# MLP down projection of a decoder layer: seven block products in place of eight

## The chip, the cores and the metric

The kernel runs on one core of a Trainium2 chip. The metric is the time of one execution in microseconds (us): the median of three runs of the kernel before is 2969.28 us (2967.07 to 2970.88).

The core has five engines with their own instruction queues: PE (TensorE, matrix products), DVE (VectorE), ACT (ScalarE), POOL (GpSimd) and SP (SyncE, which here only issues DMAs). Each queue is worked off in order; an instruction that has to wait holds up all that stand behind it on the same engine. Sixteen DMA engines move the data, whichever queue issued the transfer.

## The reference, cut to what matters

A decoder layer on 512 tokens with 2,048 features: three token mixers (a gated delta net, window attention, cross-attention to a memory), merged with gates and projected, then a squared-ReLU MLP with 8,192 hidden features. All in float32. The change is in the last line:

```python
h2 = rms_norm(x, mlp_norm_w[l])
x = x + jnp.square(jax.nn.relu(h2 @ w_mlp_up[l])) @ w_mlp_down[l]
```

`w_mlp_up` is 2048 x 8192 and `w_mlp_down` is 8192 x 2048. The output is `x`, 512 x 2048.

## The kernel before, in words

The kernel streams every weight matrix once from DRAM, in tiles of 256 rows by 512 columns (512 KB), laid out as 128 partitions x 2 x 512 in the tile `raw`. A float32 product is made of three products in a narrower form: each operand is split into a high part and a remainder, and `mm3` (L111 to L113) adds high x high, high x low and low x high into the same PSUM bank. One matmul has a 128 x 128 stationary operand and 512 moving columns.

So each weight tile goes through the same three steps before PE can use it: SP loads it (`wload`, L92; four `raw` buffers), ACT casts it into `whi` (L100; three buffers) and DVE forms the remainder `wlo` (L102; three buffers). A load waits until the buffer's last reader is done, the cast waits for a free `whi`.

The MLP runs in eight trips (`e_` from 0 to 7), each over 1,024 hidden features. In a trip, `feat_major` forms the hidden features in two halves of 512: eight weight tiles for each half, 24 matmuls for a tile, four PSUM accumulators `fa`. Each accumulator goes through ReLU on ACT (L929), a square on DVE (L930) and the split into `u_h` and `u_l` (L933, L934). Then `tok_major` runs the down projection: for each of four column groups of 512, four weight tiles of 24 matmuls each into four accumulators `ta`, one for each 128 tokens, and four DVE instructions (L939) that add the scaled accumulators to the residual `x1`. That makes 16 up tiles and 16 down tiles, 384 + 384 matmuls, in a trip. In the last trip the finished `x1` tiles are written out.

The order of instructions on each engine is set when the kernel is built, by a scheduler that puts ready instructions in the program's order as far as buffers allow. The hardware then follows that order.

Of the kernel before, what the change touches and what calls it, by code (L numbers as in the profile page):

```python
# [7 lines left out]
F32 = mybir.dt.float32  # L8
F32R = mybir.dt.float32r
BF16 = mybir.dt.bfloat16  # L10
AF = mybir.ActivationFunctionType
ALU = mybir.AluOpType
AX = mybir.AxisListType

P = 128
# [17 lines left out]
N_SLOTS = 75  # L33
YA, YB, YC, YX, YM = 10, 9, 5, 4, 14


@with_exitstack
def tile_layer(ctx: ExitStack, tc: tile.TileContext, a, out: bass.AP):
# [10 lines left out]
    def T(name, dt=F32, shape=(P, 512)):  # L49
        return big.tile(list(shape), dt, tag="T", bufs=N_SLOTS, name=name)  # L50
# [12 lines left out]

# [1 line left out]
    ident = const.tile([P, P], F32, name="ident")  # L65
# [19 lines left out]
    def rsqrt(out_ap, in_ap, n):  # L85
        nc.gpsimd.tensor_tensor(out=out_ap, in0=in_ap, in1=mhalf[:, :n], op=ALU.pow)

# [1 line left out]
    def wload(src, n):  # L89
        raw = wp.tile([P, 2, n], F32, tag="raw", bufs=4, padded_shape=[P, 2, 512], name="raw")  # L90
        if len(src.shape) == 3:
            nc.sync.dma_start(out=raw, in_=src)  # L92
        else:
            for k in range(2):
                nc.sync.dma_start(out=raw[:, k, :].rearrange("p (a b) -> p a b", b=src.shape[3]), in_=src[:, k])
        return wsplit(raw, n)
# [8 lines left out]
    def rows(w, k0, c0, n):  # L105
        return w[k0:k0 + 2 * P, c0:c0 + n].rearrange("(k p) c -> p k c", p=P)
# [8 lines left out]
    def feat_major(srcs, act, nacc):  # L115
        """out[a] = (W[:, a-th 128 columns])^T act; act[k] = (hi, lo) of [128 features, 512 tokens]."""
        accs = [acc_tile("fa") for _ in range(nacc)]
        ng_ = len(srcs)
        for g, s in enumerate(srcs):
            hi, lo = wload(s, nacc * P)  # L120
            for j in range(nacc):
                for k in range(2):
                    ah, al = act[2 * g + k]
                    c = slice(j * P, (j + 1) * P)
                    mm3(accs[j], hi[:, k, c], lo[:, k, c], ah, al, g == 0 and k == 0, g == ng_ - 1 and k == 1)
                pump()
# [21 lines left out]

# [1 line left out]
    bg = []  # L150
# [14 lines left out]

# [1 line left out]
    hm = []  # L167
# [60 lines left out]

    # remaining constants
    cm = const.tile([P, 5, P], F32, name="cm")  # L230
# [18 lines left out]

# [1 line left out]
    hT = []  # L251
# [85 lines left out]

# [1 line left out]
    toep = []  # L339
# [36 lines left out]
    for g in range(8):  # L376
        raw = wp.tile([P, 2, 268], F32, tag="raw", bufs=4, padded_shape=[P, 2, 512], name="raw")
        nc.sync.dma_start(out=raw[:, :, 0:12], in_=rows(w_in, 256 * g, COL_BA, 12))
        nc.sync.dma_start(out=raw[:, :, 12:268], in_=rows(w_in, 256 * g, COL_SK, 256))
        hi, lo = wsplit(raw, 268)  # L380
        for t in range(4):
            for k in range(2):
                ah, al = hT[2 * g + k]
                c = slice(t * P, (t + 1) * P)
                mm3(accs[t][:, :268], ah[:, c], al[:, c], hi[:, k, :], lo[:, k, :], g == 0 and k == 0, g == 7 and k == 1)
        pump()
# [17 lines left out]
    def decay():  # L404
        """beta = sigmoid(b); g = -exp(A_log) softplus(a + dt_bias); tokens on partitions."""
        bb, xa, na = th_("bb"), th_("xa"), th_("na")
# [78 lines left out]

# [1 line left out]
    def q_stats(qt):  # L487
        """rsqrt(mean(q^2) + eps) / sqrt(d) per token, [128, 4]."""
        sq = T("sq")
        nc.scalar.activation(out=sq, in_=qt, func=AF.Square)  # L490
        sp = sm("sp", (P, 4))
        for t in range(4):
            nc.tensor.matmul(sp[:, t:t + 1], lhsT=sq[:, t * P:(t + 1) * P], rhs=ones[:, 0:1], start=True, stop=True)  # L493
        ms = small("q_ms", 4, bufs=3)
        nc.vector.tensor_scalar(out=ms, in0=sp, scalar1=1.0 / HD, scalar2=EPS, op0=ALU.mult, op1=ALU.add)
        rq = small("q_r", 4, bufs=3)
        rsqrt(rq, ms, 4)
        nc.vector.tensor_scalar(out=rq, in0=rq, scalar1=SCALE, scalar2=None, op0=ALU.mult)
        return rq
# [100 lines left out]

# [1 line left out]
    def dn_head(h, raws, z, zg):  # L602
# [42 lines left out]

        # q statistics, token-major keys and values
        sq = raws[0]
# [128 lines left out]
        yield  # L776
        # chunk recurrence
        o_tok = t4(v)
# [38 lines left out]

        # gated output norm: o f rsqrt(f^2 ss / 128 + eps) w silu(z)
        f2 = small("dn_f2", 4)
# [32 lines left out]

# [1 line left out]
    merged = [None] * KT  # L854
# [34 lines left out]

# [1 line left out]
    w_out = a["w_out"][0]  # L891
# [3 lines left out]
    for c in range(4):  # L895
# [8 lines left out]
        for k in range(4):  # L904
# [7 lines left out]
            h2.append((hh, hl))  # L912
    # relu(r z)^2 = r^2 relu(z)^2, r^2 = 1 / (mean(x^2) + eps)
    r2 = const.tile([P, 4], F32, name="r2")
# [3 lines left out]

# [1 line left out]
    w_up = a["w_mlp_up"][0]  # L920
    w_dn = a["w_mlp_down"][0]
    NE = 8
    for e_ in range(NE):
        u = []
        for half in range(2):
            accs = feat_major([rows(w_up, 256 * g, e_ * 1024 + half * 512, 512) for g in range(8)], h2, 4)
            for j in range(4):
                rl = T("rl")
                nc.scalar.activation(out=rl, in_=accs[j], func=AF.Relu)  # L929
                nc.vector.tensor_tensor(out=rl, in0=rl, in1=rl, op=ALU.mult)  # L930
                hh = T("u_h", F32R)
                hl = T("u_l", F32R)
                nc.scalar.copy(out=hh, in_=rl)  # L933
                nc.vector.tensor_tensor(out=hl, in0=rl, in1=hh.bitcast(F32), op=ALU.subtract)  # L934
                u.append((hh, hl))
        for c in range(4):
            accs = tok_major([rows(w_dn, e_ * 1024 + 256 * g, c * 512, 512) for g in range(4)], u, 512, 4)
            for t in range(4):
                nc.vector.scalar_tensor_tensor(out=x1[t, c], in0=accs[t], scalar=r2[:, t:t + 1], in1=x1[t, c], op0=ALU.mult, op1=ALU.add)  # L939
                if e_ == NE - 1:  # L940
                    nc.sync.dma_start(out=out[0, t * P:(t + 1) * P, c * 512:(c + 1) * 512], in_=x1[t, c])


def _constants():
    """Index patterns that depend on the shapes alone."""
    import math
# [62 lines left out]
```

## Time and profile before

| | us |
|---|---|
| median of 3 runs | 2969.28 (2967.07 to 2970.88) |
| profiled execution, first to last instruction | 2966.8 |
| PE busy | 2946.1 (99%) |
| DVE busy | 1145.6 (39%) |
| ACT busy | 872.2 (29%) |
| POOL busy | 125.1 (4%) |

The profile gives the profiled execution's span, from its first to its last instruction; the three timed runs lie 0.3 to 4.1 us above that span. A busy share is a mean over the whole span, and matmuls overlap one another in the profile: a matmul is shown as 389 ns long, though about 1,325 of them end in 300 us. So the pace of PE is read from the count of matmuls in a stretch, not from the mean duration of one.

### The profile page before, as it was taken

The numbers are of one execution on the slowest core, as the hardware profiler recorded it, in microseconds if no ns is written. First come the engines' busy times: TensorE is split into PE (matmuls) and PEld (weight loads), VectorE is DVE, ScalarE is ACT, GpSimd is POOL, SyncE is SP. The second block draws the span as 40 slices with busy tenths as digits, with TensorE's granted clock in tenths as the row PEclk, the third lists the DMA queues.
The fourth block names the chain that finished last, engine by engine and source line by source line (L and its number), as shares of the span: only waits on it lengthen the run. The fifth ranks groups of instructions, "written<-read, shape, count | busy, mean of one in ns | idle before, by whom it ended". The sixth has DMA issues, their size and how long they took to land.

```text
span 2966.8 us, 33995 instructions
## 1 busy us (share of the span) xinstructions
PE 2946.1 (99%) x14046; PEld 2405.0 (81%) x14046; DVE 1145.6 (39%) x1697; ACT 872.2 (29%) x1352; POOL 125.1 (4%) x134
## 2 busy tenths in 40 slices
PE   8999999999999999999999999999999999999999
PEld 6988777777888888888888888888888888888887
DVE  6435666645322323343323333333332332433333
ACT  6334443344222222222323213122221312222131
POOL 0001111100000100010000000000000000000000
PEclk9999999999999999999999999999999999999999
DMA  6423222122333333333333333333333333333333
GB/s 228 119 71 87 65 68 66 54 65 65 95 97 100 93 99 100 93 98 111 113 119 93 99 94 99 98 94 100 95 97 100 93 99 100 93 100 96 96 100 106
DMA packets 198837, 285.97 MB, mean 96 GB/s; under 512 B 19575, under 2 KB 76698, under 8 KB 198682
## 3 DMA queue, kind: packets, MB, share of 16 engines
q1 hardware_dynamic: 189312, 281.16, 31.9%
q10 hardware_dynamic: 9370, 2.64, 0.4%
q8 instruction: 110, 1.80, 0.2%
q14 instruction: 45, 0.37, 0.0%
HBM read 279.16 MB, written 4.60 MB: 96 GB/s over the span
## 4 chain that ended last, share of the span: by engine, by line
PE 96%; DVE 1%; DMA 1%; POOL 1%; ACT 1%; issue 0%; ACTq 0%; SPq 0%; POOLq 0%; DVEq 0%
PE fa L111 20%; PE fa L112 20%; PE fa L113 20%; PE ta L113 10%; PE ta L111 10%; PE ta L112 10%; PE ps L802 1%; PE dps L795 1%; PE ps L810 1%; PE ps L789 0%; PE yy L754 0%; PE sp L493 0%; PE lp L561 0%; PE lp L517 0%; DVE wlo L102 0%
## 5 line engine op out<-in xcount | busy, mean ns | idle before, releaser
L102 DVE TENSOR_TENSOR wlo<-raw,whi 128x1024 fp32r<-128x1024 f32 (+2 forms) x520 | 626.7, 1206 | 1518.4 <-ACT whi L100 1514.8
L100 ACT CAST whi<-raw 128x1024 fp32r<-128x1024 f32 (+2 forms) x520 | 536.9, 1033 | 1682.7 <-PE fa L112 977.2
L111 PE MATMUL fa<-h_h,whi 128*128 128x512 f32 x2336 | 927.5, 397 | 0.0
L113 PE MATMUL fa<-h_h,wlo 128*128 128x512 f32 x2336 | 912.4, 391 | 0.0
L112 PE MATMUL fa<-h_l,whi 128*128 128x512 f32 x2336 | 912.4, 391 | 0.0
L111 PEld LDWEIGHTS fa<-h_h,whi 128*128 128x128 f32 x2336 | 438.6, 188 | 98.2 <-issue 11.3
L113 PEld LDWEIGHTS fa<-h_h,wlo 128*128 128x128 f32 x2336 | 438.5, 188 | 92.3 <-issue 1.0
L112 PEld LDWEIGHTS fa<-h_l,whi 128*128 128x128 f32 x2336 | 438.9, 188 | 86.6 <-issue 1.2
L111 PE MATMUL ta<-whi,u_h 128*128 128x512 f32 x1024 | 398.3, 389 | 0.0
L112 PE MATMUL ta<-wlo,u_h 128*128 128x512 f32 x1024 | 398.3, 389 | 0.0
L113 PE MATMUL ta<-whi,u_l 128*128 128x512 f32 x1024 | 398.3, 389 | 0.0
L113 PEld LDWEIGHTS ta<-whi,u_l 128*128 128x128 f32 x1024 | 192.2, 188 | 39.9
L111 PEld LDWEIGHTS ta<-whi,u_h 128*128 128x128 f32 x1024 | 192.2, 188 | 39.9
L112 PEld LDWEIGHTS ta<-wlo,u_h 128*128 128x128 f32 x1024 | 192.2, 188 | 39.9
L939 DVE SCALAR_TENSOR_TENSOR x<-ta,r,x 128x512 f32<-128x512 f32 x128 | 93.0, 747 | 44.2 <-PE ta L113 44.2
L111 PE MATMUL ta<-whi,m_h 128*128 128x512 f32 x256 | 99.9, 390 | 0.0
L113 PE MATMUL ta<-whi,m_l 128*128 128x512 f32 x256 | 99.6, 389 | 0.0
L112 PE MATMUL ta<-wlo,m_h 128*128 128x512 f32 x256 | 99.6, 389 | 0.0
L111 PE MATMUL fa<-ob_h,whi 128*128 128x512 f32 x256 | 99.6, 389 | 0.0
L112 PE MATMUL fa<-ob_l,whi 128*128 128x512 f32 x256 | 99.6, 389 | 0.0
L113 PE MATMUL fa<-ob_h,wlo 128*128 128x512 f32 x256 | 99.6, 389 | 0.0
L882 POOL TENSOR_TENSOR mg<-mg,sg 128x512 f32<-128x512 f32 x32 | 49.6, 1580 | 639.6 <-DVE sg L881 639.6
(279 smaller groups left out, 1912.0 us busy)
## 6 DMA issues: line engine op xcount, KB each, us to landing
raw<-in_w_mlp_up_dram SPq DMA_DIRECT2D x128, 512.0 KB, 3.7
raw<-in_w_mlp_down_dram SPq DMA_DIRECT2D x128, 512.0 KB, 3.8
raw<-in_w_in_dram SPq DMA_DIRECT2D x112, 512.0 KB, 3.6
raw<-in_w_in_dram SPq DMA_DIRECT2D x120, 256.0 KB, 3.0
raw<-in_w_out_dram SPq DMA_DIRECT2D x32, 512.0 KB, 3.8
raw<-in_w_mem_kv_dram SPq DMA_DIRECT2D x16, 512.0 KB, 4.9
raw<-in_p_swa_dram SPq DMA_DIRECT2D x12, 512.0 KB, 3.8
raw<-in_p_dn_dram SPq DMA_DIRECT2D x12, 512.0 KB, 3.8
```

Of the source, the lines that this page charges most:

```text
L100: nc.scalar.copy(out=hi, in_=raw)
L102: nc.vector.tensor_tensor(out=lo, in0=raw, in1=hi.bitcast(F32), op=ALU.subtract)
L111: nc.tensor.matmul(ps, lhsT=l_hi, rhs=r_hi, start=first, stop=False)
L112: nc.tensor.matmul(ps, lhsT=l_hi, rhs=r_lo, start=False, stop=False)
L113: last_mm[0] = nc.tensor.matmul(ps, lhsT=l_lo, rhs=r_hi, start=False, stop=last)
L795: nc.tensor.matmul(dps[rs, :], lhsT=R[rs, t, :], rhs=tmp, start=True, stop=True)
L802: nc.tensor.matmul(ps2, lhsT=kd[rs, t, :], rhs=delta, start=True, stop=True)
L810: nc.tensor.matmul(ps3[rs, :], lhsT=PT[rs, t, :], rhs=delta, start=True, stop=True)
L882: nc.gpsimd.tensor_tensor(out=merged[kt], in0=merged[kt], in1=sg[j], op=ALU.add)
L939: nc.vector.scalar_tensor_tensor(out=x1[t, c], in0=accs[t], scalar=r2[:, t:t + 1], in1=x1[t, c], op0=ALU.mult, op1=ALU.add)
```

## The change

Down projection. In seven of the eight trips, the product of the hidden features (512 tokens x 1,024 features) and the down weights (1,024 x 2,048) is cut into 2 x 2 blocks on both sides: blocks (t, k) of 256 tokens by 512 features, and blocks (k, m) of 512 features by 1,024 columns. The table `SEVEN` lists seven products of sums of blocks (`at` for the left sum, `bt` for the right sum) and the output blocks that each product is added to (`ct`, with signs), in place of the eight products of single blocks. The last trip stays with single blocks.

A product has two units (one for each group of 512 columns), a unit has two weight tiles, and a weight tile now has 12 matmuls (two groups of 128 tokens instead of four). A unit's two accumulators `da` come from the other PSUM pool.

Right-hand sums. Of the seven products, two have a difference of weight blocks (both blocks are loaded, DVE subtracts them in place), three have a sum (the first block is loaded by SP, then a DMA issued from POOL adds the second into the same tile), and two have a single block. Each of the four weight tiles of a product is loaded, summed and split on its own.

Left-hand sums. The squared hidden features `u` are kept whole (128 x 2 x 256) and are split for each product by `split`, after a DVE add or subtract where `at` has two blocks. The square is done on ACT.

Order. `merged_order` takes one step of the next trip's up projection (one weight tile, 24 matmuls) and one unit of the present trip's down projection (two weight tiles, 24 matmuls) in turn: 14 such pairs, then two up steps alone. The up steps of trip 0 stand alone at the start, the down projection of trip 7 alone at the end.

The diff, without the lines that only lose a comment or name the count of `raw` buffers:

```diff
+RAWS = 4
+SEVEN = (
+    (((0, 0, 1),), ((0, 1, 1), (1, 1, -1)), ((0, 1, 1), (1, 1, 1))),
+    (((1, 1, 1),), ((1, 0, 1), (0, 0, -1)), ((0, 0, 1), (1, 0, 1))),
+    (((0, 0, 1), (1, 1, 1)), ((0, 0, 1), (1, 1, 1)), ((0, 0, 1), (1, 1, 1))),
+    (((1, 0, 1), (1, 1, 1)), ((0, 0, 1),), ((1, 0, 1), (1, 1, -1))),
+    (((0, 0, 1), (0, 1, 1)), ((1, 1, 1),), ((0, 0, -1), (0, 1, 1))),
+    (((1, 0, 1), (0, 0, -1)), ((0, 0, 1), (0, 1, 1)), ((1, 1, 1),)),
+    (((0, 1, 1), (1, 1, -1)), ((1, 0, 1), (1, 1, 1)), ((0, 0, 1),)),
+)
...
-            for j in range(4):
-                rl = T("rl")
-                nc.scalar.activation(out=rl, in_=accs[j], func=AF.Relu)
-                nc.vector.tensor_tensor(out=rl, in0=rl, in1=rl, op=ALU.mult)
-                hh = T("u_h", F32R)
-                hl = T("u_l", F32R)
-                nc.scalar.copy(out=hh, in_=rl)
-                nc.vector.tensor_tensor(out=hl, in0=rl, in1=hh.bitcast(F32), op=ALU.subtract)
-                u.append((hh, hl))
-        for c in range(4):
-            accs = tok_major([rows(w_dn, e_ * 1024 + 256 * g, c * 512, 512) for g in range(4)], u, 512, 4)
...
+                for h in range(2):
+                    if k == 0:
+                        u[p_, h] = T("u", shape=(P, 2, 256))
+                    nc.scalar.activation(out=u[p_, h][:, k, :], in_=accs[j][:, h * 256:(h + 1) * 256], func=AF.Relu)
+                    if k == 1:
+                        nc.scalar.activation(out=u[p_, h], in_=u[p_, h], func=AF.Square)
...
+    def down_units(e_, u):
+        for at, bt, ct in SEVEN:
+            act = []
+            for i in range(2):
+                t0, k0, _ = at[0]
+                src = u[2 * k0 + i, t0]
+                if len(at) == 2:
+                    t1, k1, s1 = at[1]
+                    both = T("a_s", shape=(P, 2, 256))
+                    nc.vector.tensor_tensor(out=both, in0=src, in1=u[2 * k1 + i, t1], op=sgn[s1][0])
+                    src = both
+                act.append(split(src))
+            for c in range(2):
+                accs = [sm("da") for _ in range(2)]
+                for i in range(2):
+                    raws = []
+                    plus = len(bt) == 2 and bt[1][2] == 1
+                    for n_, (k0, m0, _) in enumerate(bt):
+                        src = rows(w_dn, e_ * 1024 + k0 * 512 + i * 256, m0 * 1024 + c * 512, 512)
+                        if n_ and plus:
+                            nc.gpsimd.dma_start(out=raws[0], in_=src, accum_op=ALU.add)
+                            continue
+                        raw = wp.tile([P, 2, 512], F32, tag="raw", bufs=RAWS, name="raw")
+                        nc.sync.dma_start(out=raw, in_=src)
+                        raws.append(raw)
+                    if len(raws) == 2:
+                        nc.vector.tensor_tensor(out=raws[0], in0=raws[0], in1=raws[1], op=ALU.subtract)
+                    hi, lo = wsplit(raws[0], 512)
+                    ah, al = act[i]
+                    for t in range(2):
+                        for k in range(2):
+                            cs = slice(t * P, (t + 1) * P)
+                            mm3(accs[t], ah[:, k, cs], al[:, k, cs], hi[:, k, :], lo[:, k, :], i == 0 and k == 0, i == 1 and k == 1)
+                for t in range(2):
+                    for t0, m0, s0 in ct:
+                        tt, cc_ = 2 * t0 + t, 2 * m0 + c
+                        nc.vector.scalar_tensor_tensor(out=x1[tt, cc_], in0=accs[t], scalar=sgn[s0][1][:, tt:tt + 1], in1=x1[tt, cc_], op0=ALU.mult, op1=ALU.add)
+                yield
+    def merged_order(first_, second):
+        live = [first_, second]
+        while live:
+            for gen in list(live):
+                if next(gen, "end") == "end":
+                    live.remove(gen)
```

In the changed program L104 is the load in `wload`, L112 the cast to `whi`, L114 the remainder `wlo`, L993 the load of a down block, L990 the adding DMA, L996 the subtraction, L966 and L979 the split and the sum of hidden features, L1006 the addition to `x1`.

What SP issues in one trip before (`raw` is the weight tile; rows of the same kind are counted):

```order
L92 DMA raw<-in_w_mlp_up_dram 128x2x512 x16
L92 DMA raw<-in_w_mlp_down_dram 128x2x512 x16
L92 DMA raw<-in_w_mlp_up_dram 128x2x512 x16
L92 DMA raw<-in_w_mlp_down_dram 128x2x512 x16
```

And now, at the start of a trip, through the units of the first product, which takes a difference (two neighbouring numbers of `raw` are the two blocks of one difference):

```order
L104 DMA raw_16159<-in_w_mlp_up_dram 128x2x512
L993 DMA raw_16199<-in_w_mlp_down_dram 128x2x512
L993 DMA raw_16201<-in_w_mlp_down_dram 128x2x512
L993 DMA raw_16220<-in_w_mlp_down_dram 128x2x512
L993 DMA raw_16222<-in_w_mlp_down_dram 128x2x512
L104 DMA raw_16245<-in_w_mlp_up_dram 128x2x512
L993 DMA raw_16277<-in_w_mlp_down_dram 128x2x512
L993 DMA raw_16279<-in_w_mlp_down_dram 128x2x512
L993 DMA raw_16298<-in_w_mlp_down_dram 128x2x512
L993 DMA raw_16300<-in_w_mlp_down_dram 128x2x512
L104 DMA raw_16323<-in_w_mlp_up_dram 128x2x512
L993 DMA raw_16363<-in_w_mlp_down_dram 128x2x512
```

Up and down loads alternate, and a unit of a difference takes four of the four buffers. By the program's waits, the load of raw_16222 goes into the buffer that the subtraction into raw_16199 frees, raw_16277 into that of the subtraction into raw_16220, raw_16298 into that of raw_16277's, raw_16363 into that of raw_16298's.

What stands on DVE in a stretch of the down projection before:

```order
L102 TENSOR_TENSOR wlo<-raw,whi 128x1024 x3
L939 SCALAR_TENSOR_TENSOR x_10793<-ta,r_11993,x_10793 128x512
L939 SCALAR_TENSOR_TENSOR x_10795<-ta,r_11993,x_10795 128x512
L939 SCALAR_TENSOR_TENSOR x_10797<-ta,r_11993,x_10797 128x512
L939 SCALAR_TENSOR_TENSOR x_10799<-ta,r_11993,x_10799 128x512
L102 TENSOR_TENSOR wlo<-raw,whi 128x1024 x4
```

And now, between the first and the second product, where `da` is a unit's accumulator, raw_16323 an up tile and raw_16363 and raw_16384 the two weight tiles of the next unit:

```order
L114 TENSOR_TENSOR wlo_16327<-raw_16323,whi_16325 128x1024
L996 TENSOR_TENSOR raw_16363<-raw_16363,raw_16365 128x1024
L966 TENSOR_TENSOR a_l_16680<-a_s_16677,a_h_16679 128x512
L979 TENSOR_TENSOR a_s_16683<-u_15559,u_16149 128x512
L1006 SCALAR_TENSOR_TENSOR x1_11693<-da_16275,r2_11993,x1_11693 128x512
L1006 SCALAR_TENSOR_TENSOR x1_11697<-da_16275,r2_11993,x1_11697 128x512
L1006 SCALAR_TENSOR_TENSOR x1_11695<-da_16276,r2_11993,x1_11695 128x512
L1006 SCALAR_TENSOR_TENSOR x1_11699<-da_16276,r2_11993,x1_11699 128x512
L114 TENSOR_TENSOR wlo_16370<-raw_16363,whi_16368 128x1024
L996 TENSOR_TENSOR raw_16384<-raw_16384,raw_16386 128x1024
L966 TENSOR_TENSOR a_l_16686<-a_s_16683,a_h_16685 128x512
L114 TENSOR_TENSOR wlo_16391<-raw_16384,whi_16389 128x1024
```

Four additions to `x1`, which wait for the last matmul of the unit before, now stand ahead of the remainders of both weight tiles of the next unit, with a subtraction and two operations on the hidden features among them.

## Rows read from the trace of the kernel before

**Rows 1.** The page: busy time by engine, then the 40 slices.

```profile
span 2966.8 us, 33995 instructions
PE 2946.1 (99%) x14046; PEld 2405.0 (81%) x14046; DVE 1145.6 (39%) x1697; ACT 872.2 (29%) x1352; POOL 125.1 (4%) x134
...
PEclk9999999999999999999999999999999999999999
DMA  6423222122333333333333333333333333333333
GB/s 228 119 71 87 65 68 66 54 65 65 95 97 100 93 99 100 93 98 111 113 119 93 99 94 99 98 94 100 95 97 100 93 99 100 93 100 96 96 100 106
```

**Rows 2.** The page: chain of waits that ended last, by engine.

```profile
PE 96%; DVE 1%; DMA 1%; POOL 1%; ACT 1%; issue 0%; ACTq 0%; SPq 0%; POOLq 0%; DVEq 0%
```

**Rows 3.** Busy time in stretches of the MLP; last three columns clock, DMA, GB/s.

```profile
core 0: us, PE busy (x) PEld busy (x) DVE busy (x) ACT busy (x) POOL busy (x), PEclk, DMA share, GB/s
...
2100.00:2400.00 300.00, 300.00 (x1325) 248.40 (x1324) 104.68 (x111) 75.55 (x87) 0.00 (x0) 1.00 0.32 97
```

**Rows 4.** Groups by line and shape in the MLP, 1580 to 2960 us.

```profile
line engine op names shapes xcount | busy us, mean ns | idle before us <-releasers
L111 PE MATMUL ta<-whi,u_h 128*128 128x512 f32 x1021 | 397.2, 389 | 0.0
...
L102 DVE TENSOR_TENSOR wlo<-raw,whi 128x1024 fp32r<-128x1024 f32 x252 | 308.7, 1225 | 828.0 <-ACT whi L100 825.8
L100 ACT CAST whi<-raw 128x1024 fp32r<-128x1024 f32 x252 | 265.5, 1054 | 977.4 <-PE ta L113 521.1 <-PE fa L112 456.3
...
L939 DVE SCALAR_TENSOR_TENSOR x<-ta,r,x 128x512 f32<-128x512 f32 x126 | 91.5, 747 | 43.0 <-PE ta L113 43.0
L934 DVE TENSOR_TENSOR u_l<-rl,u_h 128x512 fp32r<-128x512 f32 x64 | 44.2, 691 | 33.0 <-ACT u_h L933 33.0
L930 DVE TENSOR_TENSOR rl<-rl 128x512 f32<-128x512 f32 x64 | 43.9, 685 | 0.0
L933 ACT CAST u_h<-rl 128x512 fp32r<-128x512 f32 x64 | 39.8, 622 | 49.2 <-DVE rl L930 49.2
L929 ACT ACTIVATE rl<-fa 128x512 f32<-128x512 f32 x64 | 38.0, 594 | 8.5 <-PE fa L113 8.5
```

**Rows 5.** The page: DMA issues, KB each, median us from issue to landing.

```profile
raw<-in_w_mlp_up_dram SPq DMA_DIRECT2D x128, 512.0 KB, 3.7
raw<-in_w_mlp_down_dram SPq DMA_DIRECT2D x128, 512.0 KB, 3.8
...
raw<-in_w_mem_kv_dram SPq DMA_DIRECT2D x16, 512.0 KB, 4.9
...
x<-in_x_dram SPq DMA_DIRECT2D x16, 256.0 KB, 6.1
```

**Rows 6.** Busy time in stretches of the start; columns as in rows 3.

```profile
20.00:30.00 10.00, 6.59 (x37) 4.60 (x37) 6.06 (x10) 5.54 (x8) 0.00 (x0) 1.00 0.69 239
30.00:40.00 10.00, 9.43 (x36) 5.94 (x35) 5.63 (x13) 9.84 (x29) 0.56 (x1) 1.00 1.04 374
```

**Rows 7.** Waits of SP's queue in the MLP: total us, times, longest us.

```profile
SPq L92 <- DVE wlo L102: 1242.2, 250, 6.7
```

**Rows 8.** Time line of SP: the issues of four x1 loads and of weights.

```profile
1392.68 1.88 SPq L898 DMA_DIRECT2D x<-in_x_dram  x4
1396.27 38.31 SPq L92 DMA_DIRECT2D raw<-in_w_out_dram  x8
```

More of the change, by code (lines that the diff above doesn't have):

```diff
@@ L89, in wload @@
     def wload(src, n):
-        raw = wp.tile([P, 2, n], F32, tag="raw", bufs=4, padded_shape=[P, 2, 512], name="raw")
+        raw = wp.tile([P, 2, n], F32, tag="raw", bufs=RAWS, padded_shape=[P, 2, 512], name="raw")
         if len(src.shape) == 3:
@@ L376, in tile_layer @@
     for g in range(8):
-        raw = wp.tile([P, 2, 268], F32, tag="raw", bufs=4, padded_shape=[P, 2, 512], name="raw")
+        raw = wp.tile([P, 2, 268], F32, tag="raw", bufs=RAWS, padded_shape=[P, 2, 512], name="raw")
         nc.sync.dma_start(out=raw[:, :, 0:12], in_=rows(w_in, 256 * g, COL_BA, 12))
@@ L922, in tile_layer, with up_steps @@
     NE = 8
-    for e_ in range(NE):
-        u = []
+    nr2 = const.tile([P, 4], F32, name="nr2")
+    nc.vector.tensor_scalar(out=nr2, in0=r2, scalar1=-1.0, scalar2=None, op0=ALU.mult)
+    sgn = {1: (ALU.add, r2), -1: (ALU.subtract, nr2)}
+    def up_steps(e_, u):
         for half in range(2):
-            accs = feat_major([rows(w_up, 256 * g, e_ * 1024 + half * 512, 512) for g in range(8)], h2, 4)
-            for j in range(4):
-                rl = T("rl")
-                nc.scalar.activation(out=rl, in_=accs[j], func=AF.Relu)
-                nc.vector.tensor_tensor(out=rl, in0=rl, in1=rl, op=ALU.mult)
-                hh = T("u_h", F32R)
-                hl = T("u_l", F32R)
-                nc.scalar.copy(out=hh, in_=rl)
-                nc.vector.tensor_tensor(out=hl, in0=rl, in1=hh.bitcast(F32), op=ALU.subtract)
-                u.append((hh, hl))
-        for c in range(4):
-            accs = tok_major([rows(w_dn, e_ * 1024 + 256 * g, c * 512, 512) for g in range(4)], u, 512, 4)
-            for t in range(4):
-                nc.vector.scalar_tensor_tensor(out=x1[t, c], in0=accs[t], scalar=r2[:, t:t + 1], in1=x1[t, c], op0=ALU.mult, op1=ALU.add)
-                if e_ == NE - 1:
-                    nc.sync.dma_start(out=out[0, t * P:(t + 1) * P, c * 512:(c + 1) * 512], in_=x1[t, c])
@@ new lines, in up_steps @@
+            accs = [acc_tile("fa") for _ in range(4)]
+            for g in range(8):
+                hi, lo = wload(rows(w_up, 256 * g, e_ * 1024 + half * 512, 512), 512)
+                for j in range(4):
+                    for k in range(2):
+                        ah, al = h2[2 * g + k]
+                        c = slice(j * P, (j + 1) * P)
+                        mm3(accs[j], hi[:, k, c], lo[:, k, c], ah, al, g == 0 and k == 0, g == 7 and k == 1)
+                if g < 7:
+                    yield
@@ new lines, in up_steps, with split @@
+            for j in range(4):
+                p_, k = 2 * half + j // 2, j % 2
+                for h in range(2):
[4 more added lines that the diff above has]
+                        nc.scalar.activation(out=u[p_, h], in_=u[p_, h], func=AF.Square)
+            yield
+    def split(src):
+        hh = T("a_h", F32R, (P, 2, 256))
+        hl = T("a_l", F32R, (P, 2, 256))
+        nc.scalar.copy(out=hh, in_=src)
+        nc.vector.tensor_tensor(out=hl, in0=src, in1=hh.bitcast(F32), op=ALU.subtract)
+        return hh, hl
@@ new lines, in down_units @@
+    def down_units(e_, u):
[28 more added lines that the diff above has]
+                    for t in range(2):
+                        for k in range(2):
+                            cs = slice(t * P, (t + 1) * P)
[4 more added lines that the diff above has]
+                        nc.vector.scalar_tensor_tensor(out=x1[tt, cc_], in0=accs[t], scalar=sgn[s0][1][:, tt:tt + 1], in1=x1[tt, cc_], op0=ALU.mult, op1=ALU.add)
+                yield
@@ new lines, in merged_order @@
+    def merged_order(first_, second):
[4 more added lines that the diff above has]
+                    live.remove(gen)
+    u = {}
+    for _ in up_steps(0, u):
+        pass
+    for e_ in range(NE - 1):
+        nu = {}
+        merged_order(up_steps(e_ + 1, nu), down_units(e_, u))
+        u = nu
+    us = {key: split(t_) for key, t_ in u.items()}
+    e_ = NE - 1
+    for c in range(4):
+        accs = [sm("da") for _ in range(4)]
+        for g in range(4):
+            hi, lo = wload(rows(w_dn, e_ * 1024 + 256 * g, c * 512, 512), 512)
+            for t in range(4):
+                for k in range(2):
+                    ah, al = us[g, t // 2]
+                    cs = slice((t % 2) * P, (t % 2 + 1) * P)
+                    mm3(accs[t], ah[:, k, cs], al[:, k, cs], hi[:, k, :], lo[:, k, :], g == 0 and k == 0, g == 3 and k == 1)
+        for t in range(4):
+            nc.vector.scalar_tensor_tensor(out=x1[t, c], in0=accs[t], scalar=r2[:, t:t + 1], in1=x1[t, c], op0=ALU.mult, op1=ALU.add)
+            nc.sync.dma_start(out=out[0, t * P:(t + 1) * P, c * 512:(c + 1) * 512], in_=x1[t, c])
```

## Prediction

> **What bounds the kernel now.** I read the busy line and the slices first. PE is busy 99% of the span, at full granted clock in every slice, while DVE (39%), ACT (29%) and the DMA engines (3 tenths, some 97 GB/s) have room [rows 1]. The chain that ended last says the same: 96% of it is PE [rows 2]. Then the stage that the change touches. In 300 us of the MLP, PE runs 1,325 matmuls without a gap [rows 3], so one takes 300 / 1,325 = 0.2264 us; the 389 ns in the groups overlap one another [rows 4]. ACT's cast waits for PE to free a `whi` buffer (521.1 + 456.3 of its 977.4 us of idle time), DVE waits for ACT [rows 4], and SP waits 1242.2 us for DVE's remainder to free a `raw` buffer [rows 7]. The whole weight stream stands behind PE: fewer matmuls make the MLP shorter one for one, until something in the stream becomes the slower one.
>
> **What the change removes.** A trip's down projection had 384 matmuls and has 7/8 of them, 336. Over seven trips that is 336 matmuls less: 336 x 0.2264 = 76.1 us. From the profiled execution: 2966.8 - 76.1 = 2890.7 us of span; the median of the runs is 2.5 us above that span, so 2893 us if all else hides behind PE. The trip's PE time falls from 173.9 to 720 x 0.2264 = 163.0 us. A pair of an up step and a down unit has 48 matmuls, 10.87 us; an up tile 5.43 us, a down tile now 2.72 us.
>
> **What it adds, as sums.** DVE, before, in a trip: 32 remainders x 1.225 + 8 x 0.691 + 8 x 0.685 + 16 x 0.747 = 62.2 us [rows 4] (the stretch shows 104.68 in 300, the same share [rows 3]). Now: 44 remainders (16 up, 28 down) 53.9; 8 subtractions of 128 x 1024, two tiles in and one out like the remainder, 9.8; 14 splits of `u` at 0.691, 9.7; 10 sums of `u` at 0.685, 6.9; 48 additions to `x1` at 0.747, 35.9. In all 116 us of 163.0, 71%: hidden as a mean. In the two products with a difference it is tight: in a pair 3 remainders, 2 subtractions, 4 additions and a split, 9.8 us of 10.87. ACT: 44 casts x 1.054, 16 half-size ReLUs at no more than 0.594, 8 squares at 0.594, 14 casts x 0.622, together at most 69 of 163 us [rows 4]; hidden. POOL has nothing else to do there (0.00 us [rows 3]).
>
> DMA: 64 blocks of 524,288 bytes in a trip instead of 32, 33.6 MB in 163.0 us, 206 GB/s where it was 97. A pair with two blocks to a tile moves five, 241 GB/s. The start of the kernel shows 374 GB/s at a DMA share of 1.04 [rows 6], so about 360 GB/s is full, and one block costs 1.46 us of all engines. Plain loads alone thus fit: 5 x 1.46 = 7.3 of 10.87 us.
>
> **Where it may not hide.** Three places, in a trip.
>
> First, the differences. Four buffers hold two differences, and by the program's waits each second load goes into the buffer that the subtraction before it frees. Load, subtract, load, subtract is a serial chain through the four weight tiles of the first product, to the first tile of the second: four links in two pairs, so PE allows 5.43 us a link. A link is a landing and a subtraction. Landing takes 3.8 us when one load is out at a time, 4.9 us in the stage at the start, and 6.1 us where four are issued together [rows 5, 8]. The start moves 239 GB/s in one of its stretches [rows 6], as the pair will, so I take 4.9: 4.9 + 1.225 = 6.13, 0.7 over, 2.8 us a trip. By 3.8 it is 5.03 and costs nothing, by 6.1 it is 7.33 and costs 7.6 us.
>
> Second, DVE's order. Ahead of a difference's next unit stand the four additions, which wait for PE to end the unit before. From there to the second weight tile: 4 x 0.747 + 1.225 (remainder) + 1.225 (subtraction) + 1.054 (cast, on ACT) + 1.225 = 7.72 us, and PE has an up tile and a down tile in hand, 8.15 us. It fits by 0.43 us, and a split and a sum of `u` (1.4 us) stand in the same queue. I charge 0.5 us twice a trip, 1.0; the bounds are 0 and 2.8 (both in the way each time).
>
> Third, the adding DMAs. Before has none; the nearest rows are plain loads. An add can't start before its first load has landed, so a tile's buffer is held for both. The first summed tile follows the differences: its buffer is freed 4 x 0.747 + 1.225 = 4.2 us after the end of a unit, and PE comes to it three times 5.43 us after that end. Less cast and remainder (2.3 us), 9.8 us are left for load and add. For the add I take 4.9 + 1.46 = 6.4 us, a load at this traffic and one more pass for reading the tile it adds to: 4.9 + 6.4 = 11.3, 1.5 us late. Lower bound 3.8 + 3.8 = 7.6, no cost; upper 6.1 + 12.2 (two of the slowest landings) = 18.3, 8.5 us. The second summed tile has about 11.4 us, later ones more, since their buffers come free at the pace of plain splits; these hide.
>
> In engine time a pair with sums is 3 x 1.46 plus two adds. With two passes each it is 10.2 us, under 10.87; with one pass 7.3; with three 13.1. I take two passes, the middle, so no cost there. No row here shows an adding DMA. The Trainium skill (Collectives: The Full Stack, section "The bandwidth ceiling: the fold count and why AG ≠ RS ≠ AR") says that an add made by a DMA runs at about half a copy's rate, because it reads two sources; by that the pair is at 10.2 us, 94% of PE's time, and by the plain-load row at 67%. The same skill (DMA: Bandwidth & Descriptors, section "Latency and other measured facts") gives about 1 us to the first byte from GpSimd's queue against 0.6 us from SP's; by that, as an estimate, the third place costs 0.4 us more a trip.
>
> Starts and ends: trip 0's up projection and trip 7's down projection stand alone as before. At a trip's end ReLUs, squares and casts of `u` fall on ACT, but two up tiles and a unit, 16 us of PE work, cover them. Nothing for it.
>
> Sum: 2.8 + 1.0 + 1.5 = 5.3 us a trip, 37 us in seven. 2966.8 - 76.1 + 37 = 2927.7 us of span, 2930 us as a median: 1.3% faster.
>
> **Rivals.**
>
> *All hides.* Loads keep landing in 3.8 us, as in the MLP before. For it: the engines are at most 67% busy with plain blocks. Against it: the page's start, where traffic like this landed in 4.9 us. 2893 to 2900 us.
>
> *The serial chain of loads takes all.* Loads land in 6.1 us, as four together did. Then 7.6 + 1.0 + (6.1 + 7.6 - 9.8 = 3.9) = 12.5 us a trip, 87 us, 2980 us; at 5.6 us it is 2960. For it: four or five loads in flight. Against it: each waits for a buffer, so they start apart.
>
> *The adds saturate the DMA engines: slower.* An add costs three passes (two reads and a write in turn), 4.38 us of all engines. A pair with sums then takes 13.1 us instead of 10.87; there are 42 of them: 95 us, and with the first two places (27 us) 2893 + 122 = 3015 us. It decides from where the pairs lose more than (76 - 27) / 42 = 1.2 us each, so an add of 3.8 us. For it: no row excludes it, and at two passes there is only 6% of room. Against it: the adds come in runs of two and four pairs with lighter pairs between them, and a run starts with tiles in hand. With the slowest landing rate of rows 5, four x1 loads of 256 KB in 6.1 us, 3.05 us a pass, two passes cost 6.1 us and the whole 3160 us.
>
> That the change doesn't do what it says is excluded by the built program: 336 matmuls fewer, 84 DMAs on POOL.
>
> **How the numbers follow.** Forecast (2900 to 2955) 0.42; all hides 0.12; the chain of loads (2955 to 2990) 0.16; saturated adds (above 2990) 0.30. The range 2896 to 3020 leaves out some 0.04 below and 0.14 above. The likeliest's own range is 2900 to 2955. A measurement of this kernel tells about 0.2%, 6 us, from no change. Faster by more: 0.42 + 0.12 + 0.06 of the chain = 0.60; within it 0.06; slower 0.34.
>
> **What would show it.** PE's matmul count falls by 336, and in a window of the MLP its count in 300 us falls below 1,325 by about 3%. Right: PE's gaps lie at the two products with differences and at the first summed tile, released by DVE's remainder; landing of down blocks is near 5 us, of adds near 6.4; DVE is near 70% busy and the clock stays at its full level. All hides: 1,325 matmuls in every stretch. Wrong: gaps in all pairs with sums, adds landing in 10 us or more, a DMA share near 1.0 there; or gaps at single-block products, which none of my places explains.

## The result, and the profile after

| kernel | median us | range, runs | ratio to before, 95% interval |
|---|---|---|---|
| before | 2969.28 | 2966.64 to 2970.88, 5 | |
| changed | 2985.06 | 2979.32 to 2996.58, 5 | 1.0061 [1.0040, 1.0081] |

The changed kernel is 0.6% slower, 55 us over the forecast. 76 us of PE work went, and some 92 us of waits and slower matmuls came. The runs scatter more than before's, and the profiled one, with a span of 2994.5 us, lies near the slow end.

The page of the changed kernel: busy time by engine, then the slices that answer to [rows 1].

```profile
span 2994.5 us, 34660 instructions
PE 2915.0 (97%) x13710; PEld 2353.9 (79%) x13710; DVE 1471.4 (49%) x2110; ACT 1013.4 (34%) x1606; POOL 226.4 (8%) x218
...
DMA  6423222222333333333333666676766667766663
GB/s 228 116 70 87 73 60 66 56 67 65 98 99 97 94 98 99 92 100 111 120 111 100 193 162 193 183 200 194 188 194 175 195 176 192 201 181 197 172 180 106
```

PE has 336 matmuls less (14046 - 13710), as worked out, but it is busy for only 31 us less. In the last stage the DMA engines move twice what they did, at a share of 6 to 7 tenths. The chain that ended last, which was 96% PE [rows 2], now runs through DMA for a fifth of the span; the page's lines by engine and by line:

```profile
PE 66%; DMA 20%; DVE 8%; issue 2%; ACT 2%; POOL 1%; ACTq 0%; POOLq 0%; DVEq 0%
DMA raw<-in_w_mlp_down_dram 19%; PE fa L123 15%; PE fa L124 15%; PE fa L125 15%; DVE wlo L114 3%; PE da L124 3%; PE da L125 3%; PE da L123 3%; PE ta L125 2%; PE ta L123 2%; PE ta L124 2%; DVE x L1006 2%; ACT whi L112 1%; DVE raw L996 1%; PE dps L807 1%
```

The stretch of [rows 3], where PE ran 1,325 matmuls, columns as there:

```profile
2100.00:2400.00 300.00, 288.31 (x1228) 232.37 (x1227) 185.19 (x216) 110.24 (x151) 24.10 (x20) 0.98 0.68 188
```

97 matmuls are missing in 300 us, 7%, where the forecast had 3%. To see where, the third trip, cut at the starts of its seven products (difference, difference, sum, single, single, sum, sum; 96 matmuls each, 21.7 us at full pace):

```profile
2010.30:2034.80 24.50, 22.56 (x98) 17.75 (x97) 18.58 (x23) 10.19 (x17) 0.00 (x0) 1.00 0.57 180
2034.80:2056.60 21.80, 21.80 (x97) 17.95 (x96) 18.42 (x22) 6.58 (x7) 1.20 (x1) 1.00 0.69 226
2056.60:2088.20 31.60, 25.84 (x97) 20.02 (x96) 14.00 (x16) 7.03 (x7) 3.61 (x3) 0.89 0.73 180
2088.20:2110.00 21.80, 21.80 (x98) 18.04 (x97) 12.89 (x17) 11.85 (x20) 0.00 (x0) 1.00 0.50 155
2110.00:2131.70 21.70, 21.70 (x97) 18.01 (x96) 17.78 (x23) 8.71 (x10) 2.41 (x2) 1.00 0.64 163
2131.70:2153.50 21.80, 21.80 (x97) 18.03 (x97) 10.28 (x12) 5.17 (x5) 4.82 (x4) 1.00 0.86 200
2153.50:2177.50 24.00, 22.70 (x98) 17.90 (x97) 11.40 (x12) 7.05 (x7) 2.41 (x2) 1.00 0.85 217
```

The seven take 167.2 us instead of 152.1. Ten of the 15 us are in the first product with sums, which follows the differences; the rest is in the first difference and the last sum. The clock fell only in the third row, to a mean of 0.89, which is 0.11 x 31.6 = 3.5 us of full-speed time at most. (An `fa` matmul belongs to the up projection, a `da` matmul to a down unit.)

The chain of waits through the end of the second difference and that third stretch (start, us, what; L996 subtraction, L1006 additions to `x1`, L114 remainder, L112 cast):

```profile
2045.35 1.23 DVE raw L996
2046.57 2.44 DVE x L1006 x4
2049.12 1.23 DVE wlo L114
2050.37 3.92 DMA raw<-in_w_mlp_down_dram
2054.40 0.48 issue
2054.90 8.92 DMA raw<-in_w_mlp_down_dram
2063.92 1.05 ACT whi L112
2065.00 1.24 DVE wlo L114
2066.25 5.92 DMA raw<-in_w_mlp_down_dram
2072.23 0.50 issue
2072.73 9.06 DMA raw<-in_w_mlp_down_dram
2081.89 1.05 ACT whi L112
2082.97 1.24 DVE wlo L114
2084.25 0.79 PE da L124
2085.04 0.43 PE da L125
2085.47 0.43 PE da L123
```

It reads from the top: DVE's additions delay a remainder, the remainder frees a buffer, and then load, add, cast and remainder follow one another in that buffer, twice. One turn holds it from 2050.37 to 2066.24, 15.9 us, the next from 2066.25 to 2084.21, 18.0 us. They are the first and the fourth of the product's summed tiles. PE's own rows show what it waited for each (last, the idle time before the matmul and what ended it), 3.5 us and 2.2 us:

```profile
2065.02 0.49 PE L123 MATMUL da<-whi,a_h 128*128 128x512 f32 x1 [2.78 <-ACT whi L112]
2066.28 0.50 PE L124 MATMUL da<-wlo,a_h 128*128 128x512 f32 x1 [0.76 <-DVE wlo L114]
...
2082.99 0.51 PE L123 MATMUL da<-whi,a_h 128*128 128x512 f32 x1 [1.46 <-ACT whi L112]
2084.25 0.79 PE L124 MATMUL da<-wlo,a_h 128*128 128x512 f32 x1 [0.75 <-DVE wlo L114]
```

At the bottom of the chain PE works at 0.43 us a matmul instead of 0.2264: it had waited, and was then granted the lower level for a while. The wait for the first tile in pieces:

```profile
2056.00:2060.00 4.00, 4.00 (x19) 3.34 (x18) 2.25 (x4) 0.00 (x0) 1.31 (x2) 1.00 0.76 223
2060.00:2064.00 4.00, 2.24 (x10) 1.50 (x8) 0.00 (x0) 0.08 (x1) 0.00 (x0) 1.00 1.13 216
2064.00:2070.00 6.00, 4.22 (x11) 3.09 (x12) 3.58 (x3) 2.96 (x3) 1.20 (x1) 0.73 0.80 153
```

PE is idle for 1.8 of 4 us and for as much of the next 6, and the mean granted clock of those 6 us is 0.73, a mixture of its two levels (2.4 and 1.2 GHz).

DMA issues, answering to [rows 5] (KB each, median us to landing); L990 is the adding DMA, from POOL's queue:

```profile
raw<-in_w_mlp_down_dram SPq DMA_DIRECT2D x268, 512.0 KB, 4.3
raw<-in_w_mlp_up_dram SPq DMA_DIRECT2D x128, 512.0 KB, 4.0
...
raw<-in_w_mlp_down_dram POOLq DMA_DIRECT2D x84, 512.0 KB, 8.5
```

An add lands in 8.5 us, where I had taken 6.4. The queues' lines give its price in engine time:

```profile
q1 hardware_dynamic: 227392, 354.57, 38.4%
q0 software_dynamic: 22848, 44.05, 8.8%
```

8.8% of 2994.5 us over 84 adds is 3.1 us of all engines each; 38.4% over 354.57 MB is 1.70 us for a plain block (512 KB). An add costs 1.85 blocks. These are times of packets, and packets overlap: the share above goes to 1.13. So 3 x 1.70 + 2 x 3.1 = 11.4 us for a pair with sums doesn't yet say that it can't be done in 10.87 us (see e4).

### The profile page after: what moved, and what is told of

Same layout as the page of the kernel before. It is cut to its first block, busy times and chain, and to the rows that moved or that the text cites. A ratio compares the mean times of both kernels' runs of the same rounds, so it can differ in the third digit from the quotient of the medians.

```text
span 2994.5 us, 34660 instructions
## 1 busy us (share of the span) xinstructions
PE 2915.0 (97%) x13710; PEld 2353.9 (79%) x13710; DVE 1471.4 (49%) x2110; ACT 1013.4 (34%) x1606; POOL 226.4 (8%) x218
## 3 DMA queue, kind: packets, MB, share of 16 engines
q1 hardware_dynamic: 227392, 354.57, 38.4%
## 4 chain that ended last, share of the span: by engine, by line
PE 66%; DMA 20%; DVE 8%; issue 2%; ACT 2%; POOL 1%; ACTq 0%; POOLq 0%; DVEq 0%
DMA raw<-in_w_mlp_down_dram 19%; PE fa L123 15%; PE fa L124 15%; PE fa L125 15%; DVE wlo L114 3%; PE da L124 3%; PE da L125 3%; PE da L123 3%; PE ta L125 2%; PE ta L123 2%; PE ta L124 2%; DVE x L1006 2%; ACT whi L112 1%; DVE raw L996 1%; PE dps L807 1%
## 5 line engine op out<-in xcount | busy, mean ns | idle before, releaser
L114 DVE TENSOR_TENSOR wlo<-raw,whi 128x1024 fp32r<-128x1024 f32 (+2 forms) x604 | 721.9, 1206 | 1152.7 <-ACT whi L112 1149.0
L112 ACT CAST whi<-raw 128x1024 fp32r<-128x1024 f32 (+2 forms) x604 | 618.6, 1034 | 1480.3 <-PE fa L124 647.1
L123 PEld LDWEIGHTS fa<-h_h,whi 128*128 128x128 f32 x2336 | 439.3, 188 | 98.0 <-issue 11.3
L124 PE MATMUL da<-wlo,a_h 128*128 128x512 f32 x912 | 369.6, 405 | 29.7 <-DVE wlo L114 29.6
L123 PE MATMUL da<-whi,a_h 128*128 128x512 f32 x912 | 365.9, 401 | 28.8 <-ACT whi L112 28.6
L125 PE MATMUL da<-whi,a_l 128*128 128x512 f32 x912 | 364.5, 400 | 0.4
L124 PEld LDWEIGHTS da<-wlo,a_h 128*128 128x128 f32 x912 | 176.2, 193 | 83.5 <-DVE wlo L114 47.2
L123 PEld LDWEIGHTS da<-whi,a_h 128*128 128x128 f32 x912 | 176.2, 193 | 75.2 <-ACT whi L112 37.3
L125 PEld LDWEIGHTS da<-whi,a_l 128*128 128x128 f32 x912 | 176.5, 193 | 38.2 <-DVE a_l L966 2.5
L990 POOL DMA_DIRECT2D raw<-in_w_mlp_down_dram x84 | 101.4, 1215 | 1385.4 <-DMA raw<-in_w_mlp_down_dram 911.2
L1006 DVE SCALAR_TENSOR_TENSOR x<-da,r,x 128x512 f32<-128x512 f32 x280 | 196.1, 743 | 6.8 <-PE da L125 6.8
L996 DVE TENSOR_TENSOR raw<-raw 128x1024 f32<-128x1024 f32 x56 | 68.5, 1223 | 103.8 <-DMA raw<-in_w_mlp_down_dram 103.8
```

What stands on the lines that cost most here:

```text
L112: nc.scalar.copy(out=hi, in_=raw)
L114: nc.vector.tensor_tensor(out=lo, in0=raw, in1=hi.bitcast(F32), op=ALU.subtract)
L123: nc.tensor.matmul(ps, lhsT=l_hi, rhs=r_hi, start=first, stop=False)
L124: nc.tensor.matmul(ps, lhsT=l_hi, rhs=r_lo, start=False, stop=False)
L125: last_mm[0] = nc.tensor.matmul(ps, lhsT=l_lo, rhs=r_hi, start=False, stop=last)
L990: nc.gpsimd.dma_start(out=raws[0], in_=src, accum_op=ALU.add)
```

## The experiments

All start from the changed kernel but e11. "Before" is run beside each, 2967 to 2969 us.

| run | what differs | median us (range) | ratio to before, 95% |
|---|---|---|---|
| e1 | no second block in sums | 2901.13 (2898.89 to 2901.68) | 0.9774 [0.9758, 0.9791] |
| e2 | no second block at all | 2891.32 (2890.59 to 2893.34) | 0.9745 [0.9730, 0.9759] |
| e3 | sums on DVE | 2916.89 (2914.37 to 2918.34) | 0.9829 [0.9814, 0.9844] |
| e4 | six buffers | 2900.95 (2897.70 to 2901.66) | 0.9774 [0.9759, 0.9789] |
| e5 | five buffers | 2915.59 (2909.65 to 2920.98) | 0.9816 [0.9803, 0.9830] |
| e6 | six buffers, sums on DVE | 2904.40 (2901.41 to 2908.85) | 0.9785 [0.9772, 0.9799] |
| e7 | order - 1 + + - 1 + | 2962.28 (2958.08 to 2966.82) | 0.9980 [0.9970, 0.9990] |
| e8 | no second block in differences | 2908.45 (2905.53 to 2912.18) | 0.9798 [0.9785, 0.9812] |
| e9 | adds into an unread tile | 2900.50 (2899.04 to 2901.47) | 0.9769 [0.9755, 0.9782] |
| e10 | order - - 1 + + + 1 | 2951.93 (2950.03 to 2958.17) | 0.9946 [0.9933, 0.9958] |
| e11 | before with six buffers | 2968.80 (2967.41 to 2972.40) | 1.0002 [0.9993, 1.0011] |
| e12 | e10 with six buffers | 2906.23 (2904.40 to 2910.23) | 0.9790 [0.9777, 0.9804] |

In the orders, - is a difference, + a sum, 1 a single block. e1, e2, e8 and e9 leave out parts of the sums, so they don't compute the layer and serve for their times alone.

**e1, the adds left out.**

```diff
                         if n_ and plus:
-                            nc.gpsimd.dma_start(out=raws[0], in_=src, accum_op=ALU.add)
                             continue
```

> The second block of the three sums of weight blocks is left out (no adding DMA, no load in its place); the differences stay. Theory A (the adding DMAs hold a buffer for load plus add, 4 + 9 us, and slow the loads beside them): the 9 to 11 us that PE loses in the six pairs with sums of each trip go, clock dips with them, and 2 to 4 us a trip stay at the differences: 2893 + 7 x 3.5 = 2918 us (2905 to 2930). Rival B (the differences leave buffers late, so that the first tiles after them are late whatever fills them): at least 4 us stay in the pairs right after the differences, 8 us a trip in all: 2950 us or more.

2901: the adds cost 84 us, 12 a trip, and what stays over e2 is 9.8 us, 1.4 a trip at the differences, less than either theory had. Rival B falls: without adds, the pairs after the differences lose nothing.

**e2, single blocks.**

```diff
-                        if n_ and plus:
-                            nc.gpsimd.dma_start(out=raws[0], in_=src, accum_op=ALU.add)
+                        if n_:
                             continue
```

> Second blocks are left out everywhere: no adding DMA and no subtraction, 28 single blocks a trip; matmuls, splits and additions to x1 stay. Both theories: no stall is left, 2893 us (2891 to 2900), PE at 1,325 matmuls in 300 us. Above 2905 us, something that neither names (the doubled splits, the order, the additions to x1) costs time by itself.

2891.3, 75.5 us under before: the floor is as worked out (76.1). The doubled splits, the order and the additions to `x1` cost nothing by themselves; in the stretch of [rows 3] PE is back at 1,325 matmuls:

```profile
2100.00:2400.00 300.00, 300.00 (x1325) 248.43 (x1324) 180.37 (x210) 115.33 (x153) 0.00 (x0) 1.00 0.47 140
```

**e3, the sums on DVE.**

```diff
-                        if n_ and plus:
-                            nc.gpsimd.dma_start(out=raws[0], in_=src, accum_op=ALU.add)
-                            continue
...
-                        nc.vector.tensor_tensor(out=raws[0], in0=raws[0], in1=raws[1], op=ALU.subtract)
+                        nc.vector.tensor_tensor(out=raws[0], in0=raws[0], in1=raws[1], op=ALU.add if plus else ALU.subtract)
```

> The sums are formed as the differences are: both blocks loaded by SP, DVE adds in place; no adding DMA, same bytes. Theory A: every sum then costs what a difference costs, in the profile 3 us for two products, so some 7.5 us a trip for five: 2893 + 52 = 2945 us (2925 to 2960), faster than the changed kernel (2985). Rival B (the chain of buffers, not the way of adding): the chain of load and subtraction now runs through five products, and the loss is at least what it is now, 92 us: 2985 us or more.

2917: better than theory A's own figure, and far from B's. Two loads side by side and one DVE operation of 1.2 us take two buffers, but for less time than a load and an add one after the other, which took 13.5 us in the chain above (2050.37 to 2063.82). That this is why e3 is faster is argued, not measured apart.

**e4, six buffers.**

```diff
-N_SLOTS = 75
+N_SLOTS = 71
-RAWS = 4
+RAWS = 6
```

> Six raw buffers instead of four (72 KB x 2 of the big pool's slots given up: 71 instead of 75); all else as in the changed kernel, adding DMAs too. Theory C (the number of buffers decides, since a tile of a sum holds one for 14 us): the stalls go almost wholly, 2893 to 2910 us. Theory A in its strong form (the adds' rate decides): adds still land in 8 us or more and the pairs with sums still lose half of what they do now: 2935 to 2960 us.

2901, as if the adds were free. (`N_SLOTS` is the number of slots in the pool of activation tiles; four of them make room for two buffers.) They aren't faster: they land in 8.5 us as before and bring the same bytes. The stretch of [rows 3] in e4:

```profile
2100.00:2400.00 300.00, 298.48 (x1314) 246.23 (x1314) 191.93 (x217) 114.29 (x151) 24.10 (x20) 1.00 0.75 207
```

and its adds:

```profile
raw<-in_w_mlp_down_dram POOLq DMA_DIRECT2D x84, 512.0 KB, 8.5
```

In e4's third trip, the first of the last two products with sums ran at full pace (21.8 us) at a DMA share of 0.98:

```profile
2095.50:2117.30 21.80, 21.80 (x98) 18.04 (x97) 11.29 (x13) 6.33 (x6) 4.82 (x4) 1.00 0.98 231
```

So the DMA engines carry all this traffic at nearly PE's full pace, 1,314 matmuls of 1,325. Theory A in its strong form falls; theory C stands.

**e5, five buffers.** `N_SLOTS = 73`, `RAWS = 5`.

> Five raw buffers (73 slots in the big pool), all else as in the changed kernel. Theory C' (buffer time: an up tile holds a buffer some 7 us, a summed tile some 16 us for load, add, cast and remainder, so a pair with sums asks for 39 us of the 43.5 us that four buffers have in 10.87 us, and order and queues make that too little; five have 54 us): most of the stall goes, 2900 to 2920 us, nearer to six buffers (2901) than to four (2985). If the loss falls evenly with the number of buffers instead, it lies half way: about 2943 us.

2915.6: over the floor of e2, four buffers lose 94 us, five 24, six 10. The fall is not even; the fifth buffer is worth 69 us.

**e6, six buffers and sums on DVE.** The edits of e3 and e4 together.

> Sums formed on DVE as in e3 (second block by a plain load, no adding DMA), with six raw buffers. Theory C': nothing is left to wait for, 2891 to 2898 us, some 5 us under six buffers with adding DMAs (2901), since plain loads land in 4 us and DVE is still under 80% busy. Rival (with six buffers DVE's order is the bound): it is slower than adding DMAs, 2905 us or more, with PE waiting for wlo in all pairs with two blocks.

2904, and the interval overlaps that of e4: no difference between the two ways of adding is shown once there are enough buffers. My 2891 to 2898 was missed. PE's waits that are left in the MLP name DVE's remainder, at the differences that start a trip (2.4 us for up tiles and 4.6 us for down tiles in the profiled run).

**e7, another order.** The rows of `SEVEN` as difference, single, sum, sum, difference, single, sum.

> The seven products in another order: difference, single, sum, sum, difference, single, sum. Four buffers and adding DMAs as in the changed kernel. If the first sums are late because the differences ahead of them leave the buffers late, the loss halves or better: 2935 us or less. If a run of sums costs by itself with four buffers, it stays: 2965 to 2990 us.

2962, between the two: 23 us better than the changed kernel. In its profile the gaps have moved: the first sum, now after a single, loses nothing, the second loses a little, and the difference that follows the run loses most. These three products in the third trip of e7:

```profile
2047.90:2069.70 21.80, 21.80 (x98) 18.04 (x97) 11.12 (x13) 5.27 (x5) 4.81 (x4) 1.00 0.87 207
2069.70:2092.10 22.40, 22.11 (x98) 17.76 (x96) 11.86 (x14) 9.37 (x16) 2.42 (x2) 1.00 0.86 222
2092.10:2119.30 27.20, 23.04 (x97) 17.81 (x97) 22.45 (x27) 11.47 (x16) 0.00 (x0) 1.00 0.66 205
```

**e8, sums alone.**

```diff
-                        if n_ and plus:
+                        if n_ and not plus:
+                            continue
+                        if n_:
                             nc.gpsimd.dma_start(out=raws[0], in_=src, accum_op=ALU.add)
                             continue
```

> The second block of the two differences is left out (no load, no subtraction); the sums by adding DMAs stay, four buffers. Theory C' (a summed tile's long hold is the cause): PE still loses 5 to 9 us a trip in the pairs with sums, 2930 to 2955 us. Rival (the two kinds hurt only together, one after the other): 2 us a trip at most, 2907 us or less.

2908.5: 17 us over the floor, 2.4 a trip, next to the rival's 2907 and below the 2930 to 2955 of theory C' (my name for the account by buffer time). The first product with sums, here after products without a second block, loses nothing, and the last one loses:

```profile
2029.70:2051.40 21.70, 21.70 (x97) 17.97 (x96) 13.26 (x16) 6.22 (x6) 2.41 (x2) 1.00 0.77 203
...
2116.70:2140.10 23.40, 22.58 (x97) 17.86 (x96) 11.35 (x12) 7.05 (x7) 2.41 (x2) 1.00 0.83 215
```

So e1 and e8 alone cost 10 and 17 us over the floor, and both kinds together 94. The loss isn't a sum of two prices.

**e9, adds aside.**

```diff
-N_SLOTS = 75
+N_SLOTS = 71
...
+    aside = [wp.tile([P, 2, 512], F32, tag=f"aside{i}", bufs=1, name="aside") for i in range(2)]
...
-                            nc.gpsimd.dma_start(out=raws[0], in_=src, accum_op=ALU.add)
+                            landed = nc.gpsimd.tensor_copy(out=small("tick", 1), in_=raws[0][:, 0, 0:1])
+                            aside.append(aside.pop(0))
+                            with tc.issue_after(landed.ins):
+                                nc.gpsimd.dma_start(out=aside[0], in_=src, accum_op=ALU.add)
```

The four slots given up hold the two tiles that nobody reads; there are still four `raw` buffers.

> Each adding DMA is issued as in the changed kernel, once its tile's first block has landed, but adds into one of two tiles that nobody reads (the sums of weight blocks are so left out); four raw buffers. The same bytes and adds run beside the loads, but no weight tile is held for them. If the traffic is the cause (loads beside an add land in 8 us instead of 4): the loss stays large, 2950 to 2985 us. If the hold is (a buffer kept for load plus add): 2901 (as without adds) to 2920 us.

2900.5, the same as without adds. In the stretch of [rows 3], first e9, then e1:

```profile
2100.00:2400.00 300.00, 298.51 (x1313) 245.80 (x1312) 191.76 (x217) 113.21 (x150) 33.12 (x43) 1.00 0.73 207
```

```profile
2100.00:2400.00 300.00, 298.63 (x1313) 245.53 (x1312) 191.38 (x217) 112.87 (x149) 0.00 (x0) 1.00 0.54 169
```

The adds are there (DMA share 0.73 against 0.54), and they take as long to land as in the changed kernel (8.9 us in the median, against 8.5), but PE runs the same 1,313 matmuls as without them. With four buffers the traffic costs nothing; holding a weight tile through the add does.

**e10, singles between.** The rows of `SEVEN` as difference, difference, single, sum, sum, sum, single.

> Order of the products: two differences, single, three sums, single; four buffers, adding DMAs. No sum now stands next to a difference, which e7 still had at two places a trip. If the loss is made where a difference and a sum meet (alone they cost 8 and 15 us, together 92): 2905 to 2935 us. If it is made by the length of the run of sums (now six pairs on end): 2955 us or more, with the gaps in the last pairs of the run.

2952: between the two ranges, closer to the second account, and the gaps lie where that one has them. The third trip of e10, from its first product with sums to its last:

```profile
2067.70:2089.40 21.70, 21.70 (x97) 17.98 (x96) 11.90 (x14) 9.77 (x18) 4.81 (x4) 1.00 0.83 199
2089.40:2114.30 24.90, 23.23 (x98) 17.83 (x97) 17.28 (x23) 9.17 (x12) 4.82 (x4) 1.00 0.87 207
2114.30:2140.30 26.00, 23.23 (x98) 17.70 (x97) 12.14 (x13) 7.04 (x7) 2.41 (x2) 1.00 0.78 196
```

The first sum after a single is free, the second loses 3.2 us and the third 4.3. A run of sums lives on the lead that it starts with.

**e11, the kernel before with six buffers.** `N_SLOTS = 71` and six `raw` buffers in `before`.

> The kernel before with six raw buffers and 71 slots, nothing else: a control for e4. Every theory: 2969 us, no change (2964 to 2974), since PE never waits in its MLP.

2968.8: the two buffers alone bring nothing.

**e12, e10 with six buffers.**

> The order of e10 with six raw buffers and adding DMAs. If buffers are all that was short: as six buffers in the old order or a little under it, 2891 to 2901 us. If the long run of sums is bound by the DMA engines' time (10.2 of 10.87 us a pair by engine time, measured adds 3.1 us each): 2905 us or more.

2906, 5 us more than e4. The time is that of the second account, but not the place: no pair with sums loses anything now, so the long run of sums is not bound by the DMA engines' time. What is left stands at the trip's start (PE waited 11.0 us in all for remainders of up tiles there): DVE has a subtraction, which waits for its load, in the queue ahead of an up tile's remainder. In the third trip DVE sat idle for 3.8 us for such a load, and PE then for 2.9 us. Neither of my accounts had this wait.

## Why the prediction was wrong

The floor was right. 76.1 us of PE work against 75.5 measured (e2), and DVE and ACT hide as sums: DVE is busy 64% of e4's stretch, where I had 71% (in part because neighbours overlap in the profile), ACT 38% against at most 43%.

The two places at the differences were over-priced: 2.8 + 1.0 us a trip, against 1.4 where no adds follow (e1). The loads there landed in 3.9 to 4.8 us (up and down loads of these products in e1's third trip, 1975 to 2020 us, median 4.1), so the 4.9 of the start's stage was not theirs; the row of one load at a time was nearer.

The failed step is the third place. The prediction put 1.5 us a trip on the first summed tile and said of the rest: "these hide". The adds cost 12 us a trip. Two errors are in it.

One is a size. An add lands in 8.5 us in the median and not in 6.4, and a load issued beside one landed in 8.6 (the issue at 2055.05, in the chain's stretch); the shortest of the 84 adds took 5.9 us. In the chain, load and add of the first summed tile took 13.5 us where the prediction had 11.3, against 9.8 us left, and PE waited 3.5 us for the tile instead of 1.5. What the first byte from GpSimd's queue takes by itself no run here shows; the rows have issue and landing alone.

The other is the reason why the later tiles should hide, that "their buffers come free at the pace of plain splits". The fourth summed tile is loaded into the buffer of the first, which came free only at 2066.24, and PE waited 2.2 us for it. I had checked each tile against its own deadline and never summed what a pair asks of the four buffers. With the turns of the chain above, a pair with sums asks for 2 x 15.9 to 18.0 us and an up tile for at least 3.8 + 1.05 + 1.22 = 6.1 us, 38 to 42 us in all. Four buffers have 4 x 10.87 = 43.5 us. There is little slack for any wait of a cast or a DVE queue, so a late tile frees its buffer late, and the next load and add in it are late as well. Six buffers have 65 us, and the stall is gone (e4); e9 frees the buffers without taking a byte away, and it is gone too. So the hold of a buffer through its add is shown to be the cause. The estimate of 38 to 42 us is not the price of it: the pairs with sums in e8 ask for as much, and e8 loses 2.4 us a trip.

No single price explains the rest: differences alone cost 10 us and sums alone 17, together 94 (e1, e8). What fits is an account by lead, that is by tiles that are ready before PE needs them. Each kind lives on lead gathered elsewhere; next to each other, one spends what the other needs. The order moves the gaps (e7, e10) and doesn't remove them. This account is worked out from the runs and was not tested by itself; how much of the 94 us is lateness handed on and how much a lasting shortage was not measured apart.

A part of the loss is the clock, which the prediction kept at its full level. The profiled execution had a mean granted clock of 0.991, before 0.999: 0.008 x 2994.5 = 24 us of full-speed time. Part of it falls in time in which PE waited, so it is at most 24 of some 104 us in that execution. The runs of the changed kernel scatter more than all others, with mean granted clocks of 0.990 to 0.993; that the dips cause the scatter was not tested.

Of the rivals, "saturated adds" named the place, the pairs with sums, but another way to it and a longer time (3015 us). It needed 3.8 us of all engines for an add; it is 3.1, some two passes, as I had taken. The Trainium skill (Collectives: The Full Stack, section "The bandwidth ceiling: the fold count and why AG ≠ RS ≠ AR") has a reduce step at half a copy's rate; the 1.85 blocks measured here agree with that. Two passes fit, as e4 and e9 show. "The serial chain of loads" had the range in which the time fell (2955 to 2990, to which I gave 0.16), but by luck, since it had not the place: of the two products with differences in the third trip only the first loses anything, 2.8 us, and e1 bounds both at 1.4 us a trip. "All hides" is nearly what six buffers give: 2901 us, 2.3% faster than before, the version to keep.

## What to carry to other kernels

When a step is put between a load and its use, sum the buffer time: each tile's hold (landing, the added step, its readers) over all tiles of a period, against buffers times period. Near 100% it can fail even where every engine has room in the mean. How much is then lost depends on the order too (e7, e8, e10) and doesn't follow from the sum. What helped here was a buffer more (e5, e4), or a sum formed by DVE from two loads side by side in place of an add behind the load (e3). A deadline for each tile by itself doesn't find this.

## What the hardware showed that I had not expected

An adding DMA's landing and its engine time are different things: its packets took 3.1 us of all engines, but it needed 5.9 to 11.4 us to land, and plain loads beside adds landed in up to 10.0 us instead of 3.8.

A short wait can cost twice. After waits of 2.8 and 0.8 us with one matmul between them, PE's matmuls came 0.43 us apart instead of 0.2264. But not each wait does: the start of the kernel before, with PE busy 6.59 of 10 us [rows 6], kept the full level, and so did e10's second and third sum above, in which PE was idle for 1.7 and 2.8 us.
